# Weights split two blocks ahead instead of three, token copies in GpSimd's queue, and one softmax for four chunks

## The chip, the cores and the metric

The kernel runs on one core of a Trainium2 chip. The metric is the device time of one execution in microseconds (us). Five engines with a queue each work side by side: TensorE (PE; its weight loads are listed as PEld), VectorE (DVE), ScalarE (ACT), GpSimd (POOL) and SyncE (SP), which here only issues transfers. An engine takes its instructions in the order of its own queue, and a wait at the front of a queue holds back everything behind it.

## The reference

Two layers, each a mixer (a linear recurrence in layer 0, attention in layer 1) and a feed-forward part that picks experts, on 512 tokens of 1024 numbers. The change touches the feed-forward part, which is the same in both layers:

```python
def peer_ffn(h, q_w, subkey1, subkey2, expert_u, expert_v):     # for each chunk xc of 128 tokens
    q = (xc @ q_w).reshape(128, 8, 2, 128)
    s1, s2 = q[:, :, 0] . subkey1, q[:, :, 1] . subkey2          # 8 heads x 128 keys, twice
    v1, i1 = lax.top_k(s1, 16); v2, i2 = lax.top_k(s2, 16)
    cand = v1[..., :, None] + v2[..., None, :]                   # 256 sums for each head
    top_s, top_c = lax.top_k(cand, 16)
    expert = i1[top_c // 16] * 128 + i2[top_c % 16]              # one of 16384
    g = softmax(top_s)
    act = gelu(einsum('thkd,td->thk', expert_u[expert], xc))
    return einsum('thk,thkd->td', g * act, expert_v[expert])
```

## The kernel before

**Numbers in two parts.** Every product is made of three matmuls: a float32 operand is split into a rounded part (`hi`, ScalarE, line 189) and the rest (`lo`, VectorE, or GpSimd in one stage, line 191), and hi·hi, lo·hi and hi·lo are added in PSUM. Weights come in blocks of 128 x 1024 numbers. `Stream` loads two blocks with one transfer (SP), splits them one by one and hands them out with `take`. At a `take`, it first records the splits of all blocks up to `ahead` blocks beyond the one that is taken. The split parts (`whi`, `wlo`) live in a ring of four buffers, so the split of a block cannot start before TensorE is done with the block four places before it.

**The feed-forward part, `peer`.** Four chunks of 128 tokens. For chunks 0 to 2 all 16384 experts are computed (the dense way), with a gate that is zero for experts that weren't picked; the last 32 of these 384 tokens have their 128 products with `expert_u` looked up row by row instead (`looked_up`), so the dense products with `u` have 352 columns. Chunk 3 is looked up wholly (`gathered`). There are 128 expert blocks; for 34 of the 64 pairs of blocks the products with `u` are made early and stored in DRAM, for the other 30 within the last loop. The stages, one after the other:

1. Queries: scores, the 16 best of each side, the 16 best sums.
2. Routing: `route` finds for each chunk the expert numbers (`e1`, `e2`) and the softmax (`gt`) of the picked scores. For chunk 2 it also makes `ei`; then `looked_up` copies the indices of the 32 tokens to four groups of 32 partitions (`eix`, four small transfers), their rows of h to the same groups (`hn`, three transfers), fetches rows of `expert_u` by GpSimd (`rowx`, `two`), multiplies them on VectorE and copies the result back (`back`, four transfers).
3. Gates: `dense_gates` transposes `e1`, `e2` and `gt` on TensorE and builds the gate of every expert, beside the early products with `u`.
4. The expert sum: for each pair of blocks, VectorE multiplies the products by the gates (line 1332), ScalarE rounds them (`wh`, 1335), VectorE makes the rest (`wl`, 1340), and TensorE adds them times `v` (1347), 18 matmuls of 512 columns a block. If the pair six blocks on isn't stored, 24 matmuls of 352 columns for each of its blocks stand between (556 to 558). In the background VectorE works through chunk 3: 128 products with rows of `u` (`rows`, 1235), then 128 with rows of `v` (`accg`, 1249).

**What sets the order.** The program says what is to be done and what depends on what. A scheduler then orders the instructions of each engine by estimates of its own; only those marked `keep_in_program_order` keep their place among each other. `ahead` and the length of an instruction thus move others too.

## Time and profile before

| | |
|---|---|
| time, median of 3 runs | 3040.61 us (3040.06 to 3040.77) |
| profiled execution: time, span | 3042.44 us, 3040.4 us |
| PE busy | 2964.9 us (98%) |
| DVE busy | 2563.0 us (84%) |
| ACT busy | 1451.8 us (48%) |
| POOL busy | 1157.9 us (38%) |
| granted TensorE clock, mean | 0.992 |

In the profiled execution, layer 0's routing begins at about 438 us, its gates at 470, its expert sum at 720 (rows of `u` in the background until about 1120, then rows of `v`), and ends at 1464. Layer 1's come at 2000, 2030, 2280, 2680 and 3022.

A wait row reads: engine and line that waited, the instruction it waited for, us in total, how many times, the longest. A row of the windows reads: stretch, its length, the busy time of PE, PEld, DVE, ACT and POOL with counts, the granted TensorE clock (1.00 is full), the share of the DMA engines, GB/s. A timeline row: start, duration, engine, line, operation, tiles, and in brackets the idle time ahead of it and what ended it.

### The profile page before, as it was taken

What the parts mean: (1) busy time and instruction counts of PE and PEld (TensorE: products, weight loads), DVE (VectorE), ACT (ScalarE), POOL (GpSimd) and SP (SyncE); (2) the same over time, 40 slices, a digit from 0 to 9 for tenths busy, and PEclk for the clock granted to TensorE, in tenths of its full rate; (3) what the DMA queues carried; (4) which work ended last, traced back from release to release, by engine and by line L of the source; (5) the groups of instructions that cost most, each with busy time, mean ns of one, the idle gap of its engine ahead of it and who ended that gap; (6) DMA issues with size and microseconds to landing.
All of it is one profiled execution on the core that took longest, in us unless ns stands there. A gap on an engine that the chain in (4) does not pass through costs nothing.

```text
span 3040.4 us, 44431 instructions
## 1 busy us (share of the span) xinstructions
PE 2964.9 (98%) x16232; PEld 2605.4 (86%) x16232; DVE 2563.0 (84%) x4951; ACT 1451.8 (48%) x2300; POOL 1157.9 (38%) x906
## 2 busy tenths in 40 slices
PE   7999999999999999999999999999999999999998
PEld 5778899999888888888777778899998888888887
DVE  7876989995988888888779878899977898898887
ACT  6665564664333333333468843365663333333332
POOL 1002953201765645554011004631105565554551
PEclk9999999999999999999999999999999999999999
DMA  7455558998999999988332134377998999999995
GB/s 291 174 177 198 210 182 348 303 296 310 385 364 364 395 359 380 368 334 333 112 117 84 63 153 162 140 266 279 314 303 343 396 360 362 377 385 364 353 347 199
DMA packets 306843, 855.22 MB, mean 281 GB/s; under 512 B 26208, under 2 KB 161408, under 8 KB 267840
## 3 DMA queue, kind: packets, MB, share of 16 engines
q1 hardware_dynamic: 72464, 407.65, 35.2%
q0 software_dynamic: 93440, 336.11, 29.2%
q10 hardware_dynamic: 140720, 108.63, 10.8%
q8 instruction: 127, 2.08, 0.3%
q14 instruction: 92, 0.75, 0.1%
HBM read 767.93 MB, written 83.51 MB: 280 GB/s over the span
## 4 chain that ended last, share of the span: by engine, by line
PE 69%; DVE 16%; issue 8%; ACT 4%; DMA 2%; POOL 1%; DVEq 0%; ACTq 0%; SPq 0%; POOLq 0%
PE vacc L1347 27%; PE pacc L556 11%; PE pacc L557 10%; PE pacc L558 10%; DVE accg L1249 2%; PE gps L1179 2%; DVE wlo L191 2%; ACT whi L189 1%; DVE pg L1206 1%; DVE rows L1235 1%; DVE wl L1340 1%; PE oacc L600 1%; PE oacc L599 1%; PE oacc L601 1%; DMA wraw<-in_l_uT_dram 1%
## 5 line engine op out<-in xcount | busy, mean ns | idle before, releaser
L189 ACT ACTIVATE whi<-wraw 128x1024 fp32r<-128x1024 f32 (+1 forms) x646 | 669.0, 1039 | 893.8 <-PE vacc L1347 387.6
L191 DVE TENSOR_TENSOR wlo<-wraw,whi 128x1024 fp32r<-128x1024 f32 (+2 forms) x580 | 697.6, 1211 | 332.4 <-ACT whi L189 331.1
L556 PE MATMUL pacc<-hhi,whi 128*128 128x352 f32 (+1 forms) x2600 | 890.6, 343 | 0.6 <-issue 0.6
L558 PE MATMUL pacc<-hhi,wlo 128*128 128x352 f32 (+1 forms) x2600 | 883.1, 340 | 1.5 <-DVE wlo L191 1.5
L557 PE MATMUL pacc<-hlo,whi 128*128 128x352 f32 (+1 forms) x2600 | 882.8, 340 | 0.0
L1347 PE MATMUL vacc<-whi,wh 128*128 128x512 f32 x1536 | 601.0, 391 | 0.0
L1347 PE MATMUL vacc<-wlo,wh 128*128 128x512 f32 x1536 | 599.2, 390 | 0.0
L1347 PE MATMUL vacc<-whi,wl 128*128 128x512 f32 x1536 | 564.3, 399 | 22.0 <-DVE wl L1340 21.3
L557 PEld LDWEIGHTS pacc<-hlo,whi 128*128 128x128 f32 x2600 | 491.6, 189 | 26.6
L556 PEld LDWEIGHTS pacc<-hhi,whi 128*128 128x128 f32 x2600 | 490.3, 189 | 27.2 <-issue 0.9
L558 PEld LDWEIGHTS pacc<-hhi,wlo 128*128 128x128 f32 x2600 | 490.1, 188 | 26.3 <-DVE wlo L191 2.5
L1222 POOL DMA_INDIRECT rows<-in_l_v_dram,ei x256 | 369.6, 1444 | 348.0 <-DVE accg L1249 275.2
L1222 POOL DMA_INDIRECT rows<-in_l_u_dram,ei x256 | 409.3, 1599 | 242.7 <-DVE rows L1235 179.3
L1347 PEld LDWEIGHTS vacc<-whi,wl 128*128 128x128 f32 x1536 | 287.5, 190 | 100.3 <-DVE wl L1340 40.9
L1347 PEld LDWEIGHTS vacc<-whi,wh 128*128 128x128 f32 x1536 | 289.7, 189 | 57.5 <-ACT wh L1335 0.6
L1347 PEld LDWEIGHTS vacc<-wlo,wh 128*128 128x128 f32 x1536 | 290.0, 189 | 56.7
L1249 DVE SCALAR_TENSOR_TENSOR accg<-rows,act,accg 128x1024 f32<-128x1024 f32 x254 | 326.3, 1285 | 3.1
L1235 DVE SCALAR_TENSOR_TENSOR rows<-rows,hn 128x1024 f32<-128x1024 f32 x256 | 302.3, 1220 | 2.8 <-issue 2.8
L1335 ACT ACTIVATE wh<-at 128x768 fp32r<-128x768 f32 x128 | 108.2, 845 | 237.2 <-DVE at L1332 226.6
L191 POOL TENSOR_TENSOR wlo<-wraw,whi 128x1024 fp32r<-128x1024 f32 (+1 forms) x62 | 125.4, 2042 | 87.0 <-ACT whi L189 84.4
L1084 POOL DMA_INDIRECT rowx<-in_l_u_dram,eix x36 | 59.6, 1654 | 240.4 <-DVE rowx L1102 153.6
L1340 DVE TENSOR_TENSOR wl<-at,wh 128x768 fp32r<-128x768 f32 x128 | 121.8, 951 | 1.8 <-ACT wh L1335 1.8
(343 smaller groups left out, 3676.3 us busy)
## 6 DMA issues: line engine op xcount, KB each, us to landing
wraw<-in_l_uT_dram SPq DMA_DIRECT2D x128, 1024.0 KB
wraw<-in_l_vp_dram SPq DMA_DIRECT2D x128, 1024.0 KB
gscr<-st ACTq DMA_DIRECT2D x48, 1024.0 KB
gtile<-gscr SPq DMA_DIRECT2D x90, 512.0 KB
ascr<-at ACTq DMA_DIRECT2D x136, 176.0 KB
at<-ascr ACTq DMA_DIRECT2D x68, 352.0 KB
mw<-in_l_ffn_mw_dram POOLq DMA_DIRECT2D x32, 512.0 KB
wraw<-in_l_qw_dram SPq DMA_DIRECT2D x16, 1024.0 KB
```

The source lines that it names most:

```text
L189: self.pin(nc.scalar.activation(hi, raw, AF.Copy))
L191: self.pin((nc.gpsimd if self.on_pool else nc.vector).tensor_sub(lo, raw, hi))
L556: nc.tensor.matmul(ps, whi[:, k, :], hhi[:, k, :n], start=(k == 0), stop=False))
L557: nc.tensor.matmul(ps, whi[:, k, :], hlo[:, k, :n], start=False, stop=False)
L558: nc.tensor.matmul(ps, wlo[:, k, :], hhi[:, k, :n], start=False, stop=(k == KD - 1))
L1179: m = T.matmul(gps[:, r, :], p2[:, tk_, :, :].rearrange("p a b -> p (a b)"), pg[:, i].rearrange("p a (t b) -> p a t b", b=8)[:, :, tk_, :] ...
L1222: i = nc.gpsimd.indirect_dma_start(out=rows, out_offset=None, in_=src, in_offset=bass.IndirectOffsetOnAxis(ap=ei[:, j:j + 1], axis=0))
L1235: V.scalar_tensor_tensor(r, r, 1.0, hn, op0=OP.mult, op1=OP.mult, accum_out=act[:, j:j + 1]))
L1249: i = V.scalar_tensor_tensor(acc, r, w, acc, op0=OP.mult, op1=OP.add)
L1335: (pin if c < 2 else lambda x: x)(A.activation(wh, at, AF.Copy))
L1340: return lambda: pin(V.tensor_sub(wl, at, wh))
L1347: T.matmul(acc[t][d], x[:, ts], y[:, d, :], start=(i == 0 and x is wh and y is vh), stop=(i == PK - 1 and x is wl))
```

## The change

Three edits, in both layers:

- `ahead` stays at two for the expert sum's loop and goes back to three only behind it. (The gate stage had two before.)
- The copies of `eix`, `hn` and `back` are issued in GpSimd's queue, not in ScalarE's: eleven transfers in each layer.
- The softmax is made once for all four chunks, when the first chunk has been routed: one subtraction, one exponential, one sum and one reciprocal of four times the length; the last multiplication stays with each chunk.

```diff
+        def weights():
+
+            ex = env["exp"] = rs.tile([128, TC, PH, TOPK], F32, name="exps")
+            V.tensor_tensor(ex, top, top[:, :, :, 0:1].to_broadcast([128, TC, PH, TOPK]), op=OP.subtract)
+            A.activation(ex, ex, AF.Exp)
+            gs = env["sum"] = rs.tile([128, TC, PH], F32, name="sums")
+            V.tensor_reduce(gs, ex, axis=AX.X, op=OP.add)
+            V.reciprocal(gs, gs)
+
         def route(t):
...
             e = routes[t]
+            if t == nd - 1:
+                weights()
             gt = (rt if t < nd else pk).tile([128, PH, TOPK], F32, name="gt", tag="gt_", bufs=3 if t < nd else 1)
-            V.tensor_tensor(gt, top[:, t], top[:, t, :, 0:1].to_broadcast([128, PH, TOPK]), op=OP.subtract)
-            A.activation(gt, gt, AF.Exp)
-            gs = rt.tile([128, PH], F32, name="gs", tag="gs")
-            V.tensor_reduce(gs, gt, axis=AX.X, op=OP.add)
-            V.reciprocal(gs, gs)
-            V.tensor_tensor(gt, gt, gs.unsqueeze(2).to_broadcast([128, PH, TOPK]), op=OP.mult)
+            V.tensor_tensor(gt, env["exp"][:, t], env["sum"][:, t].unsqueeze(2).to_broadcast([128, PH, TOPK]), op=OP.mult)
...
             def groups(to, of):
                 for s in range(SG):
-                    nc.scalar.dma_start(to[s * XT:(s + 1) * XT], of[own, s * XT:(s + 1) * XT])
+                    nc.gpsimd.dma_start(to[s * XT:(s + 1) * XT], of[own, s * XT:(s + 1) * XT])
...
             for s in range(SG - 1):
-                nc.scalar.dma_start(hn[s * XT:(s + 1) * XT], hn[own])
+                nc.gpsimd.dma_start(hn[s * XT:(s + 1) * XT], hn[own])
...
             for s in range(SG):
-                nc.scalar.dma_start(back[own, s * XT:(s + 1) * XT], act[s * XT:(s + 1) * XT])
+                nc.gpsimd.dma_start(back[own, s * XT:(s + 1) * XT], act[s * XT:(s + 1) * XT])
...
                     bg.pump(GP)
                 bg.finish()
-                g.stream.ahead = 3
...
             bg.finish()
+            g.stream.ahead = 3
             gguard.__exit__(None, None, None)
```

**The order at the expert sum.** VectorE's queue in layer 0, in the part with rows of `v`, ahead of one `wl`. A block's two parts are `whi_N` and the `wlo` numbered one higher; numbers grow in the order of the program and differ between the two builds. Before, where `wl_12416` belongs to the pair that begins with block 12383:

```order
L1249 SCALAR_TENSOR_TENSOR accg_8337<-rows_12417,act_8336,accg_8337 128x1024
L191 TENSOR_TENSOR wlo_12421<-wraw_12381,whi_12420 128x1024
L191 TENSOR_TENSOR wlo_12427<-wraw_12424,whi_12426 128x1024
L1249 SCALAR_TENSOR_TENSOR accg_8337<-rows_12451,act_8336,accg_8337 128x1024
L1249 SCALAR_TENSOR_TENSOR accg_8337<-rows_12454,act_8336,accg_8337 128x1024
L1249 SCALAR_TENSOR_TENSOR accg_8337<-rows_12457,act_8336,accg_8337 128x1024
L191 TENSOR_TENSOR wlo_12496<-wraw_12424,whi_12495 128x1024
L1249 SCALAR_TENSOR_TENSOR accg_8337<-rows_12460,act_8336,accg_8337 128x1024
L1340 TENSOR_TENSOR wl_12416<-at2_12250,wh_12414 128x768
```

The same place in the changed kernel, where `wl_12396` belongs to the pair that begins with block 12402:

```order
L1255 SCALAR_TENSOR_TENSOR accg_8319<-rows_12397,act_8318,accg_8319 128x1024
L191 TENSOR_TENSOR wlo_12403<-wraw_12400,whi_12402 128x1024
L191 TENSOR_TENSOR wlo_12407<-wraw_12400,whi_12406 128x1024
L1255 SCALAR_TENSOR_TENSOR accg_8319<-rows_12431,act_8318,accg_8319 128x1024
L1255 SCALAR_TENSOR_TENSOR accg_8319<-rows_12434,act_8318,accg_8319 128x1024
L1255 SCALAR_TENSOR_TENSOR accg_8319<-rows_12437,act_8318,accg_8319 128x1024
L191 TENSOR_TENSOR wlo_12478<-wraw_12475,whi_12477 128x1024
L1255 SCALAR_TENSOR_TENSOR accg_8319<-rows_12440,act_8318,accg_8319 128x1024
L1345 TENSOR_TENSOR wl_12396<-at2_12230,wh_12394 128x768
```

The kinds of instructions are the same; each split is now that of the block one place earlier (before, those of blocks one, two and three behind 12383; now those of 12402 itself and the next two).

TensorE's queue at the block that first needs this `wl`, before:

```order
L1347 MATMUL vacc20_8067<-whi_12383,wh_12414 128x512
L1347 MATMUL vacc20_8067<-wlo_12384,wh_12414 128x512
L1347 MATMUL vacc21_8068<-whi_12383,wh_12414 128x512
L1347 MATMUL vacc21_8068<-wlo_12384,wh_12414 128x512
L1347 MATMUL vacc00_8063<-whi_12383,wl_12416 128x512
L1347 MATMUL vacc01_8064<-whi_12383,wl_12416 128x512
```

and now:

```order
L1352 MATMUL vacc00_8049<-whi_12402,wh_12394 128x512
L1352 MATMUL vacc00_8049<-wlo_12403,wh_12394 128x512
L1352 MATMUL vacc01_8050<-whi_12402,wh_12394 128x512
L1352 MATMUL vacc01_8050<-wlo_12403,wh_12394 128x512
L1352 MATMUL vacc10_8051<-whi_12402,wh_12394 128x512
L1352 MATMUL vacc00_8049<-whi_12402,wl_12396 128x512
```

Before, all twelve matmuls of the block that don't need `wl` stood ahead of the first that does; now five do. There are 64 `wl` in each layer; the rows `wlo`, three times `accg`, `wlo`, `accg`, `wl` stand ahead of one seven times in each layer, before and now.

**The order at routing.** ScalarE's queue in layer 0, before:

```order
L876 ACTIVATE at<-pacc 128x352
L1003 ACTIVATE tab_4802<-d_4798 128x1024
L877 DMA ascr<-at 128x352
L1065 DMA eix<-ei 32x32 x4
L299 ACTIVATE hn<-nat 128x512 x2
L876 ACTIVATE at<-pacc 128x352
L1092 DMA hn<-hn 32x1024 x3
L877 DMA ascr<-at 128x352
L189 ACTIVATE whi<-wraw 128x1024
```

and now:

```order
L189 ACTIVATE whi<-wraw 128x1024
L876 ACTIVATE at<-pacc 128x352
L1003 ACTIVATE tab_4805<-idxs_2606 128x1024
L877 DMA ascr<-at 128x352
L299 ACTIVATE hn<-nat 128x512 x2
L1003 ACTIVATE tab_4803<-d_4799 128x1024
L189 ACTIVATE whi<-wraw 128x1024
```

The seven transfers are gone from between `hn` and the next weight split, `whi`; in GpSimd's queue they now stand ahead of and among the first `rowx`. TensorE's queue at the first transposes of the gate stage, before:

```order
L556 MATMUL pacc_5028<-hhi_2330,whi_4941 128x352
L557 MATMUL pacc_5028<-hlo_2331,whi_4941 128x352
L1158 MATMUL tp_5796<-ident_86,e0_4795 128x128
L1158 MATMUL tp_5796<-ident_86,e1_4796 128x128
L558 MATMUL pacc_5028<-hhi_2330,wlo_4942 128x352
```

and now:

```order
L558 MATMUL pacc_5742<-hhi_2330,wlo_5659 128x352
L1164 MATMUL tp_5782<-ident_86,e0_4796 128x128
L1164 MATMUL tp_5782<-ident_86,e1_4797 128x128
L1164 MATMUL tp_5782<-ident_86,gt_5096 128x128
L556 MATMUL pacc_5801<-hhi_2330,whi_5702 128x352
```

The transposes of `e1` and `e2` of chunk 0 stand 430 rows later now, beside that of its `gt`, which kept its place.

## The prediction

> **What bounds the kernel now.** I began with the page's busy rows and groups, then took the waits of TensorE stage by stage, the timeline of one place at which it waits, and the windows behind such places.

> ```profile
> PE 2964.9 (98%) x16232; PEld 2605.4 (86%) x16232; DVE 2563.0 (84%) x4951; ACT 1451.8 (48%) x2300; POOL 1157.9 (38%) x906
> L1347 PE MATMUL vacc<-whi,wl 128*128 128x512 f32 x1536 | 564.3, 399 | 22.0 <-DVE wl L1340 21.3
> ```

> TensorE is busy for 98% of the span of 3040.4 us, and none of the edits removes a matmul. So the change can only be worth what TensorE loses in the stages that it touches. The second row names the largest such loss: 21.3 us of waiting for `wl`. The waits of TensorE in the two expert sums (720 to 1464 and 2280 to 3022) place it:

> ```profile
> PE vacc L1347 <- DVE wl L1340: 10.4, 6, 3.0
> PE vacc L1347 <- DVE wl L1340: 10.9, 7, 2.7
> ```

> What makes `wl` late is seen in the timeline of the place whose order is shown above, with the rows of PE, ACT and DVE:

> ```profile
> 1237.64 0.39 PE L1347 MATMUL vacc<-whi,wh 128*128 128x512 f32 x1
> 1244.21 0.39 PE L1347 MATMUL vacc<-wlo,wh 128*128 128x512 f32 x1
> 1247.62 0.50 PE L1347 MATMUL vacc<-whi,wl 128*128 128x512 f32 x1 [3.02 <-DVE wl L1340]
> 1238.17 1.06 ACT L189 ACTIVATE whi<-wraw 128x1024 fp32r<-128x1024 f32 x1 [2.43 <-issue]
> 1239.27 1.22 DVE L191 TENSOR_TENSOR wlo<-wraw,whi 128x1024 fp32r<-128x1024 f32 x1 [3.08 <-ACT whi L189]
> 1240.41 3.92 DVE L1249 SCALAR_TENSOR_TENSOR accg<-rows,act,accg 128x1024 f32<-128x1024 f32 x3
> 1244.24 1.22 DVE L191 TENSOR_TENSOR wlo<-wraw,whi 128x1024 fp32r<-128x1024 f32 x1
> 1245.38 1.32 DVE L1249 SCALAR_TENSOR_TENSOR accg<-rows,act,accg 128x1024 f32<-128x1024 f32 x1
> 1246.62 0.94 DVE L1340 TENSOR_TENSOR wl<-at,wh 128x768 fp32r<-128x768 f32 x1
> ```

> At 1237.64 TensorE begins a block, and so frees the buffer of the block before. ACT can then split into it (1238.17), DVE idles 3.08 us for that, makes `wlo` (1239.27), four `accg`, another `wlo`, and only then `wl` (1246.62). TensorE goes on at 1247.62, 9.98 us after it freed the buffer. It wanted to at 1244.21 + .23 = 1244.44, since matmuls of 512 columns start .2267 us apart in these rows. So DVE wasn't short of time before this; a split that could not start sooner stood ahead of `wl`.

> The windows tell what follows a wait: stretch, length, then PE, PEld, DVE, ACT, POOL and the granted clock.

> ```profile
> 1244.40:1247.70 3.30, 0.28 (x2) 0.08 (x1) 3.30 (x4) 0.04 (x1) 2.41 (x3) 1.00 1.01 412
> 1248.90:1252.40 3.50, 3.50 (x10) 2.72 (x9) 3.46 (x4) 1.47 (x2) 2.19 (x2) 0.51 1.02 426
> 1358.10:1361.60 3.50, 3.50 (x10) 2.73 (x9) 3.08 (x4) 1.90 (x2) 1.98 (x2) 0.51 0.90 345
> 1443.40:1446.90 3.50, 3.49 (x8) 2.75 (x9) 3.30 (x3) 1.43 (x2) 0.00 (x0) 0.51 0.55 234
> 2808.80:2812.30 3.50, 3.50 (x10) 2.74 (x9) 3.25 (x4) 1.90 (x2) 1.98 (x2) 0.51 1.02 425
> 2918.00:2921.50 3.50, 3.23 (x8) 2.58 (x9) 3.46 (x4) 1.37 (x3) 1.98 (x2) 0.51 0.89 324
> 3003.40:3006.90 3.50, 3.08 (x8) 2.47 (x8) 3.46 (x4) 0.96 (x2) 0.00 (x0) 0.51 0.64 260
> ```

> Behind each of the three longest waits of each layer the granted clock is .51 for 3.50 us, while TensorE is busy. That costs 3.50 x .49 = 1.71 us each, 6 x 1.71 = 10.3 us in all, which the waits don't count. [...]

> **The change: splits two blocks ahead.** The same row of instructions stands on DVE ahead of `wl`, seven times in each layer, so from the release of the buffer to TensorE's start I keep 9.98 us. The split that begins it is now that of one block nearer, whose buffer comes free one block sooner as seen from the block that is running. Before, TensorE had from the release one block of 18 matmuls and 12 of the next until it wanted `wl`: 18 x .2267 + 12 x .2267 = 6.80 us. Now it has two blocks and five matmuls, as the second pair of order rows shows: 36 x .2267 + 5 x .2267 = 9.29 us. The wait at such a place falls from 3.18 to 9.98 − 9.29 = .69 us. I take it for all 14 places: 14 x .69 = 9.7 us remain, and 21.3 − 9.7 = 11.6 us go. The ends are 0 left (21.3 saved) and, if the four places in each layer that hardly wait now keep to that, and the scheduler's other changes undo half of it, some 6 us saved. A wait of .7 us is far below the 2.5 us or so behind which dips stand, so the six dips go: **10.3 us**. For that the window at the other end is evidence: the 1.6 us wait at 2624.5 leaves the clock at 1.00.

> ```profile
> 2624.50:2628.00 3.50, 3.46 (x16) 2.92 (x17) 3.13 (x4) 1.36 (x3) 2.03 (x2) 1.00 0.96 363
> ```

> The other face of this edit is that splits have one block less of lead. The nearest rows are a pair of splits and the block that needs it:

> ```profile
> 824.85 2.35 DVE L191 TENSOR_TENSOR wlo<-wraw,whi 128x1024 fp32r<-128x1024 f32 x2
> 827.65 0.32 PE L556 MATMUL pacc<-hhi,whi 128*128 128x352 f32 x1
> ```

> The pair ends .45 us before TensorE needs it. I take 0 for its loss, since such splits wait for the release of their buffer and not for their place in the program; the other end is one `wlo` late at each of the 60 pairs that aren't stored, and is a rival below.

> **Routing.** The waits of TensorE at 438 to 470 (three rows) and at 2000 to 2030 (two), and what ACT does ahead of the first:

> ```profile
> PE tp L1158 <- DVE e L989: 1.6, 1, 1.6
> PE pacc L558 <- DVE wlo L191: 0.8, 1, 0.8
> PE pacc L556 <- issue: 0.6, 1, 0.6
> PE tp L1158 <- DVE ge L986: 2.5, 1, 2.5
> PE pacc L558 <- DVE wlo L191: 0.7, 1, 0.7
> 450.88 2.56 ACTq L1065 DMA_DIRECT2D eix<-ei  x4
> 454.60 3.12 ACTq L1092 DMA_DIRECT2D hn<-hn  x3
> 458.41 1.06 ACT L189 ACTIVATE whi<-wraw 128x1024 fp32r<-128x1024 f32 x1 [3.48 <-issue]
> 463.80:467.30 3.50, 3.50 (x15) 3.50 (x14) 3.50 (x6) 0.15 (x1) 3.03 (x2) 0.51 1.04 410
> 2020.30:2027.20 6.90, 6.12 (x20) 5.83 (x21) 6.62 (x10) 0.88 (x1) 5.68 (x5) 0.51 1.01 393
> ```

> The seven issues hold ACT for 2.56 + 3.12 = 5.68 us, and the next weight split starts behind them after 3.48 us without work; TensorE waits .6 for it. Then the transposes of the experts' numbers stand ahead of the products and wait 1.6 and 2.5 us for VectorE, which also puts `wlo` behind. Now the issues have left ACT, and the transposes stand 430 rows later, where their `gt` had kept the gates anyway. I take all five waits, 1.6 + .8 + .6 + 2.5 + .7 = 6.2 us, and the two dips: 3.50 x .49 = 1.7 and 6.90 x .49 = 3.4. The dips are 5.1 us; together **11.3 us**. The low end is 0, if DVE's work reaches TensorE late by another way.

> **The copies in GpSimd's queue.** No such small copy is issued by POOL before. The nearest rows are its issues of other plain transfers, and its indirect fetches, with min, median and max in ns:

> ```profile
> L217 POOL DMA_DIRECT2D mw<-in_l_ffn_mw_dram x32 | 17.2, 538 | 197.7 <-DVE mw L224 131.8 <-DVE col_l_ffn L231 28.3 <-DVE ptl L304 22.8
> L1084 POOL DMA_INDIRECT rowx<-in_l_u_dram,eix x36: 936/1331/2752, 455.5 to 2160.8; - x36
> 455.54 1.15 POOL L1084 DMA_INDIRECT rowx<-in_l_u_dram,eix  x1 [32.24 <-DMA eix<-ei]
> 462.76 1.22 DVE L1102 SCALAR_TENSOR_TENSOR rowx<-rowx,hn 128x1024 f32<-128x1024 f32 x1
> ```

> Eleven issues at .54 us are 6 us a layer, in a queue that stood idle 32.24 us ahead of the first `rowx`. Behind the `hn` copies stand the fetches, and behind the fetches only the products `rowx` on DVE. Three `hn` copies among three fetches, at .54 and 1.33 us, take 5.6 us from 455.5 on: they are out at about 461, and DVE came to its first `rowx` at 462.76. So I take 0. At 2.75 us, the longest of these rows, the six would end at 472; DVE would stand some 9 us at `rowx` with splits queued behind, and the 11.3 us of routing would go back. [...]

> **One softmax.** It saves three of four rounds in each layer:

> ```profile
> L1044 ACT ACT_TABLE_LOAD x8 | 10.3, 1283 | 0.1
> ```

> Six table loads of 1.28 us go from ACT, which is busy 48%, and some short operations from DVE. No wait of TensorE above names either; 0, and with the ACT cover gone at most 6 x 1.28 = 7.7 us of gain.

> **Sum.** 11.6 + 10.3 + 11.3 = 33.2 us. The profiled execution took 3042.44 us, 1.83 above the median of 3040.61 (2.0 around its span). 3042.4 − 33.2 = 3009.2; against the median, 3040.6 − 33.2 = **3007 us**. If all that is listed went, 21.3 + 10.3 + 11.3 = 42.9, it would be 2998.

> **Rivals.**

> *VectorE is the bound at these places.* While TensorE waits, DVE is busy for 3.30 of 3.30 us (first window). Were its work simply too much there, a sooner release would only move the wait, dips included, and routing alone would gain: 3040.6 − 11.3 = 3029. For it speaks the row of the rows-of-`v` stretch:

> ```profile
> 1120.00:1464.00 344.00, 335.03 (x1601) 287.87 (x1600) 293.17 (x261) 122.17 (x164) 163.05 (x116) 0.99 0.89 342
> ```

> Against it: 293 of 344 us is 85%, and the idle 3.08 us stands directly ahead of the long run.

> *Nothing comes of it.* As before, and the copies by POOL take 2.75 us, so that routing gives back its gain as well; that is about 3040, at most a few us below.

> *Slower: splits come late.* With one block less of lead each pair that isn't stored finds its second `wlo` behind one more DVE instruction, 1.22 us, of which the .45 us of margin covers a part: .77 us at 60 pairs is 46 us, minus the 33 gained: 3053. It decides from a mean lateness of 33.2 / 60 = .55 us. For it speaks the thin margin; against it, that TensorE shows no wait for `wlo` in either expert sum, and that DVE idles for `whi`, which comes by release.

> *All of it goes:* 2998, if the four other places in each layer catch up and the .69 us is covered.

> **How the numbers follow.** Chances: the forecast .62, DVE as the bound .15, nothing .08, slower .10, all of it .05. Within 0.2%, 6.1 us, a measurement of this kernel can hardly be told from no change. Faster by more come the forecast, DVE as the bound and all of it: .82; the same .08; slower .10. The range goes from 2997, all of it, to 3031, which takes in DVE as the bound: .62 + .15 + .05 = .82. The forecast's own range is 3000 to 3018.

> **What would show it.** Right: the waits for `wl` sum to some 10 us, none over 1 us; no window of clock .51 in either expert sum; no wait at the transposes; the first `rowx` on DVE near 463. Wrong: waits of 2.5 us and dips at the same count (DVE the bound); new waits of `pacc` for `wlo` in the expert sums (slower); DVE idle at `rowx` for a DMA (the copies). What I couldn't price from any row is how else the scheduler moves instructions once lengths change.

## The result, and the profile after

The changed kernel takes 2996.53 us (median of 4 runs, 2995.56 to 3000.91), where the kernel before took 3040.61. The ratio is 0.9858, with a 95% interval of 0.9841 to 0.9875: 38 to 48 us less. The forecast was 3007 us with a range down to 2997; the time lies half a microsecond below that end, and next to the rival "all of it goes" (2998), though not by that rival's way, as is shown below.

The page's busy rows of the changed kernel, and its row for the products that waited for `wl`:

```profile
PE 2943.4 (98%) x16232; PEld 2597.3 (87%) x16232; DVE 2560.1 (86%) x4933; ACT 1436.0 (48%) x2282; POOL 1196.9 (40%) x928
L1352 PE MATMUL vacc<-whi,wl 128*128 128x512 f32 x1536 | 594.7, 391 | 0.9
```

TensorE does the same 16232 matmuls, and the 21.3 us of waiting for `wl` are no longer there. The span is 46.6 us shorter (3040.4 to 2993.8). Where from is seen if both traces are cut at the same instructions: the first score product of the queries, the first product with `v`, and the last.

| us | before | after |
|---|---|---|
| layer 0: queries, routing, gates | 429.1 | 427.4 |
| layer 0: expert sum | 753.3 | 733.7 |
| layer 1: queries, routing, gates | 430.8 | 427.6 |
| layer 1: expert sum | 753.4 | 733.6 |

The expert sums gave 19.6 + 19.8 = 39.4 us, routing and gates 1.7 + 3.2 = 4.9. The rest, some 2 us, lies at the start and in the mixers, which the change doesn't touch; 1.7 of it is a dip of the clock at 1822 that is gone (last section). The expert sums end at 1475 and 3035 before, 11 and 13 us later than the stage times given ahead. Their windows, before:

```profile
721.00:1475.00 754.00, 743.28 (x3592) 641.16 (x3591) 635.36 (x712) 274.53 (x371) 395.76 (x268) 0.99 0.91 352
2281.00:3035.00 754.00, 742.72 (x3592) 641.05 (x3591) 633.07 (x704) 269.46 (x358) 391.85 (x265) 0.99 0.91 351
```

and after:

```profile
718.00:1452.00 734.00, 733.51 (x3590) 638.00 (x3590) 634.61 (x712) 273.65 (x370) 406.05 (x268) 1.00 0.93 360
2254.00:2988.00 734.00, 733.54 (x3590) 637.96 (x3589) 631.73 (x704) 268.69 (x358) 404.57 (x265) 1.00 0.93 360
```

VectorE does the same work (635.36 and 634.61 us) in 20 us less, and TensorE is busy throughout, at the full clock. So VectorE's load was not the bound.

The place whose order stands in the chapter on the change, in the timeline of the changed kernel, rows of PE, ACT and DVE:

```profile
1224.51 0.39 PE L1352 MATMUL vacc<-whi,wh 128*128 128x512 f32 x1
1233.59 0.39 PE L1352 MATMUL vacc<-whi,wh 128*128 128x512 f32 x1
1234.01 0.50 PE L1352 MATMUL vacc<-whi,wl 128*128 128x512 f32 x1
1224.55 1.06 ACT L189 ACTIVATE whi<-wraw 128x1024 fp32r<-128x1024 f32 x1 [2.11 <-PE pacc L557]
1225.64 1.23 DVE L191 TENSOR_TENSOR wlo<-wraw,whi 128x1024 fp32r<-128x1024 f32 x1 [1.95 <-ACT whi L189]
1226.79 3.92 DVE L1255 SCALAR_TENSOR_TENSOR accg<-rows,act,accg 128x1024 f32<-128x1024 f32 x3
1230.63 1.22 DVE L191 TENSOR_TENSOR wlo<-wraw,whi 128x1024 fp32r<-128x1024 f32 x1
1231.76 1.32 DVE L1255 SCALAR_TENSOR_TENSOR accg<-rows,act,accg 128x1024 f32<-128x1024 f32 x1
1233.01 0.95 DVE L1345 TENSOR_TENSOR wl<-at,wh 128x768 fp32r<-128x768 f32 x1
```

From `whi` to TensorE's first matmul with `wl` it still takes 9.46 us (before 9.45). What changed is that this chain begins when two blocks and five matmuls lie ahead of that matmul. It is .2 us late here (1234.01, where 1233.59 + .23 = 1233.82 would be prompt), not 3.18.

Routing and the gates are where less came than forecast. The waits of TensorE there, two in each layer, and the windows behind the second of each:

```profile
PE gps L1185 <- DVE pg L1212: 2.1, 1, 2.1
PE pacc L558 <- DVE wlo L191: 0.7, 1, 0.7
PE gps L1185 <- DVE pg L1212: 1.9, 1, 1.9
PE pacc L558 <- DVE wlo L191: 1.2, 1, 1.2
538.20:541.60 3.40, 3.40 (x28) 3.40 (x26) 3.40 (x5) 2.53 (x5) 0.47 (x1) 0.54 0.55 169
2074.20:2077.60 3.40, 3.30 (x33) 3.30 (x32) 3.40 (x6) 1.79 (x3) 0.00 (x0) 0.54 0.49 131
```

The waits at the transposes are gone, but two others are not. The first gate product now waits 2.1 and 1.9 us (1.1 before in both layers), and the clock halves behind it in both layers. And a split is still late, by .7 and 1.2 us (.8 and .7 before), in layer 0 by this chain of rows of POOL, DVE and PE:

```profile
458.80 0.57 POOL L1098 DMA_DIRECT2D hn<-hn  x1
465.00 1.23 DVE L1108 SCALAR_TENSOR_TENSOR rowx<-rowx,hn 128x1024 f32<-128x1024 f32 x1 [1.23 <-DMA hn<-hn]
471.95 1.22 DVE L191 TENSOR_TENSOR wlo<-wraw,whi 128x1024 fp32r<-128x1024 f32 x1
473.23 0.43 PE L558 MATMUL pacc<-hhi,wlo 128*128 128x352 f32 x1 [0.65 <-DVE wlo L191]
```

GpSimd issued the last copy of `hn` in .57 us and was done at 459.4 (the prediction had 461), but VectorE could start on it only at 465.0, some 5.6 us after the issue ended. VectorE stood 1.23 us for it (1.88 in layer 1), then another .41 and .47 us for rows fetched for `two`, and the `wlo` that TensorE waits for stands behind these.

### The profile page after: what moved, and what is told of

The parts are those of the page before. It is cut to its first block, busy times and chain, and to the rows that moved or that the text cites. A ratio compares the mean times of both kernels' runs of the same rounds, so it can differ in the third digit from the quotient of the medians.

```text
span 2993.8 us, 44407 instructions
## 1 busy us (share of the span) xinstructions
PE 2943.4 (98%) x16232; PEld 2597.3 (87%) x16232; DVE 2560.1 (86%) x4933; ACT 1436.0 (48%) x2282; POOL 1196.9 (40%) x928
## 3 DMA queue, kind: packets, MB, share of 16 engines
q10 hardware_dynamic: 139664, 107.77, 11.3%
## 4 chain that ended last, share of the span: by engine, by line
PE 74%; DVE 13%; issue 6%; ACT 3%; DMA 2%; POOL 1%; DVEq 0%; SPq 0%; ACTq 0%; POOLq 0%
PE vacc L1352 32%; PE pacc L556 10%; PE pacc L557 10%; PE pacc L558 10%; PE gps L1185 2%; DVE wlo L191 2%; DVE pg L1212 1%; DVE accg L1255 1%; ACT whi L189 1%; DMA mw<-in_l_mix_mw_dram 1%; PE oacc L601 1%; PE oacc L600 1%; PE oacc L599 1%; DMA two<-in_l_u_dram,eix 1%; DVE rowx L1108 1%
## 5 line engine op out<-in xcount | busy, mean ns | idle before, releaser
L189 ACT ACTIVATE whi<-wraw 128x1024 fp32r<-128x1024 f32 (+1 forms) x646 | 668.7, 1038 | 906.5 <-PE pacc L557 423.5
L191 DVE TENSOR_TENSOR wlo<-wraw,whi 128x1024 fp32r<-128x1024 f32 (+2 forms) x580 | 697.2, 1211 | 287.7 <-ACT whi L189 283.3
L556 PE MATMUL pacc<-hhi,whi 128*128 128x352 f32 (+1 forms) x2600 | 889.4, 342 | 0.0
L558 PE MATMUL pacc<-hhi,wlo 128*128 128x352 f32 (+1 forms) x2600 | 882.4, 340 | 2.0 <-DVE wlo L191 1.9
L1352 PE MATMUL vacc<-whi,wl 128*128 128x512 f32 x1536 | 594.7, 391 | 0.9
L558 PEld LDWEIGHTS pacc<-hhi,wlo 128*128 128x128 f32 x2600 | 489.0, 188 | 29.0 <-DVE wlo L191 6.6
L1228 POOL DMA_INDIRECT rows<-in_l_u_dram,ei x256 | 419.9, 1640 | 230.0 <-DVE rows L1241 165.6
L556 PEld LDWEIGHTS pacc<-hhi,whi 128*128 128x128 f32 x2600 | 489.5, 188 | 25.6 <-ACT at L876 0.2
L1228 POOL DMA_INDIRECT rows<-in_l_v_dram,ei x256 | 382.0, 1492 | 317.9 <-DVE accg L1255 249.2
L1255 DVE SCALAR_TENSOR_TENSOR accg<-rows,act,accg 128x1024 f32<-128x1024 f32 x254 | 325.9, 1283 | 2.9
L1340 ACT ACTIVATE wh<-at 128x768 fp32r<-128x768 f32 x128 | 108.4, 846 | 196.4 <-DVE at L1337 186.5
L191 POOL TENSOR_TENSOR wlo<-wraw,whi 128x1024 fp32r<-128x1024 f32 (+1 forms) x62 | 124.8, 2026 | 85.4 <-ACT whi L189 82.7
```

The source lines that it names most:

```text
L189: self.pin(nc.scalar.activation(hi, raw, AF.Copy))
L191: self.pin((nc.gpsimd if self.on_pool else nc.vector).tensor_sub(lo, raw, hi))
L556: nc.tensor.matmul(ps, whi[:, k, :], hhi[:, k, :n], start=(k == 0), stop=False))
L558: nc.tensor.matmul(ps, wlo[:, k, :], hhi[:, k, :n], start=False, stop=(k == KD - 1))
L1228: i = nc.gpsimd.indirect_dma_start(out=rows, out_offset=None, in_=src, in_offset=bass.IndirectOffsetOnAxis(ap=ei[:, j:j + 1], axis=0))
L1255: i = V.scalar_tensor_tensor(acc, r, w, acc, op0=OP.mult, op1=OP.add)
```

## Experiments: which edit does it

**The first edit alone.**

```diff
 (kernel before)
                 bg.finish()
-                g.stream.ahead = 3
 ...
             bg.finish()
+            g.stream.ahead = 3
             gguard.__exit__(None, None, None)
```

> Only the first edit. Theory A (the late release of the split's buffer is what made wl late): the two expert sums lose what they lost in the changed kernel, 753.3 to some 734 us each, so 2 x 19.6 = 39 us: 3001 us, no wait for wl over 0.5 us, no window of clock 0.51 in either expert sum; routing as before, with its five waits and its dips. Rival B (the other two edits, by moving instructions, made room on VectorE): the waits for wl stay near 21 us and the time is over 3025 us.

Measured: 3002.45 us, ratio 0.9879 (0.9863 to 0.9896), 32 to 42 us gained. The expert sums took 733.6 and 733.5 us; their windows:

```profile
724.00:1458.00 734.00, 733.57 (x3597) 638.21 (x3596) 634.90 (x713) 273.52 (x370) 395.85 (x268) 1.00 0.94 360
2262.00:2995.00 733.00, 732.58 (x3586) 637.30 (x3587) 631.27 (x703) 268.21 (x357) 398.65 (x265) 1.00 0.93 360
```

Theory A holds: this edit by itself takes the waits for `wl` and the dips out. Routing and gates stay at 429.7 and 430.6.

**The change without the first edit**, three blocks ahead again, the other two edits kept.

> The changed kernel with three blocks ahead in the expert sum again. Theory A: 39 us come back, 3036 us, with some 13 waits for wl (21 us) and six dips of the clock. Rival B: under 3012 us, waits for wl mostly gone.

Measured: 3031.32 us, ratio 0.9972 (0.996 to 0.9983). The waits for `wl` in the two expert sums are back, and five dips with them (a sixth wait had none):

```profile
PE vacc L1353 <- DVE wl L1346: 8.7, 5, 2.7
PE vacc L1353 <- DVE wl L1346: 10.9, 9, 2.7
```

It came out some 5 us below the expectation. The expert sum of layer 0 took 749.8 us, not 753.3, and that of layer 1 753.5; so the other edits moved something in layer 0 too, a little.

**The second edit alone**: `nc.gpsimd.dma_start` for `nc.scalar.dma_start` at the eleven copies, nothing else.

> Only the second edit; the first transposes of the gate stage move back by 430 rows with it, as in the change. Theory A: what the two layers gained from the start of the queries to the end of the gates, some 5 us, and nothing else: 3035 us; VectorE waits about 1.2 us for the copy of hn, the waits at the transposes are gone, a wait of some 2 us at the first gate product takes their place. Rival (the copies by GpSimd cost more than ACT's issues did): 3041 us or more.

Measured: 3033.47 us, ratio 0.9981 (0.9972 to 0.9991): 3 to 9 us gained. Queries to gates took 427.5 and 428.2 us, as in the changed kernel, the expert sums 752.1 and 751.9. The expected wait at the first gate product did not come; the waits of `pacc` for `wlo` in routing came to 4.9 us instead.

**The change with the copies back in ScalarE's queue**, so the first and the third edit.

> The changed kernel with the eleven copies in ScalarE's queue again; the transposes stay where the change has them. Theory C (the queue edit gains nothing by itself, the move of the transposes gained): 2994 to 2998 us, no wait of VectorE for hn. Rival D (the seven issues on ACT hold back whi and TensorE): TensorE waits 0.5 us or more for a split in each layer, and dips follow: 2999 to 3003 us.

Measured: 3008.11 us, ratio 0.9903 (0.9887 to 0.992), above both expectations; the profiled span was 3002.3, 8.5 us over the changed kernel's. Queries to gates took 430.7 and 432.9 us (427.4 and 427.6), the expert sums 733.4 and 733.6. So rival D holds: the queue edit does gain. In the timeline of layer 0, rows of ACT, DVE and PE:

```profile
453.55 3.10 ACTq L1098 DMA_DIRECT2D hn<-hn  x3
458.34 2.01 ACT L189 ACTIVATE whi<-wraw 128x1024 fp32r<-128x1024 f32 x2 [0.54 <-ACT at L876]
463.49 1.22 DVE L1108 SCALAR_TENSOR_TENSOR rowx<-rowx,hn 128x1024 f32<-128x1024 f32 x1 [0.87 <-DMA rowx<-in_l_u_dram,eix]
464.64 1.22 DVE L191 TENSOR_TENSOR wlo<-wraw,whi 128x1024 fp32r<-128x1024 f32 x1
465.91 0.43 PE L558 MATMUL pacc<-hhi,wlo 128*128 128x352 f32 x1 [3.95 <-DVE wlo L191]
```

The issues hold `whi` back to 458.34; the `wlo` of a later block then falls behind a `rowx` on VectorE that waits for its own rows. With the transposes out of the way TensorE runs into this wait of 3.95 us (3.98 in layer 1) instead of theirs. How much of it is the late `whi` and how much the place of the `wlo` behind `rowx`, these rows don't tell.

**The third edit alone**: one softmax for four chunks.

> Only the third edit. The transposes of the gate stage move back with it too. Theory C (its own cost or gain is only in that move; with ACT's seven issues still there TensorE waits for splits in place of the transposes, as in the run with the copies back in ScalarE's queue): from the start of the queries to the end of the gates 430.7 and 432.9 us as there, 3.6 more than before, expert sums as before at 753: 3044 us, a ratio of 1.001. Rival (one softmax frees VectorE and ScalarE for the routing): below 3035 us, a ratio under 0.998.

Measured: 3042.28 us, ratio 1.0009 (0.9999 to 1.0018): no gain. Queries to gates took 430.3 and 431.8 us, with `pacc` waits for `wlo` of 8.0 us, the longest 4.4: theory C holds there. The expert sums took 751.8 and 748.5 us, the second 4.9 less than before, with two of its three dips gone (2806.9 and 2915.4 have the wait and no dip); theory C had not said so.

**The change without the third edit**, so the first two.

> The changed kernel with a softmax for each chunk, so the first two edits. Theory C: the same as the changed kernel within 2 us (expert sums 734 us, queries to gates as with the queue edit alone, 427.5 and 428.2): ratio 0.985 to 0.987. Rival (the softmax carries part of the gain): over 0.988.

Measured: 2997.64 us, ratio 0.9861 (0.9845 to 0.9877), the same as the changed kernel within the noise: no gain of the softmax can be seen. The expert sums took 733.9 and 733.8 us. Queries to gates took 424.1 and 429.4 us, not the 427.5 and 428.2 expected: without the third edit layer 0 was faster than in the changed kernel and layer 1 slower.

## Experiments: the release of the buffer

The first two runs show that `ahead` does it, not why. The theory says that the split's buffer came free too late; the rival, that the split stood too early in VectorE's queue. A fifth buffer frees it sooner at the same `ahead`.

**Five split buffers, paid for with row buffers (inconclusive).** In the kernel before, every fifth block of the expert sum is split into a buffer of its own, and eight buffers for looked-up rows become six. Its control has the six row buffers alone.

> The kernel before, three blocks ahead, but a ring of five buffers for the split parts in the expert sum (every fifth block in a buffer of its own), paid for by six row buffers for the looked-up rows in place of eight. Theory A (the release of the buffer is what is late): a split three ahead now waits for the block five places before it, which is released one block sooner, as with two ahead and four buffers: the waits for wl fall below 5 us, no dips in the expert sums, some 39 us gained beside its control: ratio about 0.988. Rival E (what counts is where the split stands in VectorE's queue, not when its buffer is free): waits for wl near 20 us, ratio over 0.995.

> Control of the run with five buffers: the kernel before with six row buffers in place of eight and four split buffers. Theory A: the waits for wl stay near 20 us; between 3038 and 3046 us (fewer rows in flight gain nothing), ratio 0.999 to 1.002. Rival: if fewer row buffers alone move the waits for wl below 10 us, the run with five buffers shows nothing.

Measured: 3036.47 us with five split buffers (ratio 0.9988, 0.9976 to 1.0) and 3058.94 for the control (1.0062, 1.0046 to 1.0079). The pair shows nothing on the question. With six row buffers alone the waits for `wl` in the part with rows of `v` fell to 2.6 and 2.3 us, as the rival of the control had it, but those in the part with rows of `u` rose to 15.3 and 16.7, which neither it nor the expectation had. Besides, VectorE waited 9.1 and 7.7 us for a transfer of the gate stage (`gscr`) ahead of a split, once in each layer; that the added buffer took over memory which this transfer still read is my reading.

**Five split buffers, paid for with a raw weight buffer.** All row buffers stay, and the fifth buffer is used from the fifth pair until 16 blocks before the end:

```diff
 (kernel before)
-            sp = self.spare or g.wsp
+            sp = self.spare or (self.fifth if len(self.parts) % 5 == 4 else None) or g.wsp
 ...
-            g.stream.third = (pk, vw)
+            g.stream.third = (pk,)
 ...
+                if i == 8:
+                    g.stream.fifth = fifth
                 if i == PK - 16:
                     g.stream.third = None
+                    g.stream.fifth = None
```

> The kernel before, three blocks ahead, with a fifth buffer for the split parts from the fifth pair of the expert sum on; all eight row buffers stay, and it is paid for by the raw weight buffer that the last stage had in addition (three in place of four). Theory A (the buffer's late release is the cause): in the part with rows of v (1120 to 1464, 2680 to 3022) the waits for wl fall from 8.7 and 8.4 us to under 2, without dips; expert sums some 15 us shorter each than in its control; ratio about 0.989. Rival E (the place of the split in VectorE's queue): waits there of 7 us or more, as before, ratio over 0.996.

The control has three raw buffers and four split buffers:

> Control of the run with five split buffers: the kernel before with three raw weight buffers in the expert sum in place of four. Theory A: waits for wl in the parts with rows of v stay at 8 us, with dips; 3038 to 3045 us. Rival: waits for a weight load appear (over 5 us), or the waits for wl there move below 4 us by themselves; then the pair shows nothing.

Measured: 3021.68 us with the fifth buffer (ratio 0.995, 0.9934 to 0.9967), 3040.14 for the control (1.001, 0.9999 to 1.0021). The expert sums took 742.1 and 742.4 us against 751.2 and 753.2. The waits of TensorE in the parts with rows of `v` (1110 to 1460, 2660 to 3010), control first, then with five buffers:

```profile
PE vacc L1347 <- DVE wl L1340: 8.4, 4, 2.7
PE vacc L1347 <- DVE wl L1340: 8.9, 5, 2.7
```

```profile
PE vacc L1349 <- DVE wl L1342: 2.7, 1, 2.7
PE vacc L1349 <- DVE wl L1342: 2.7, 1, 2.7
```

Two of the three long waits of each layer are gone, and the one that remains, in layer 0 at 1428 to 1431, lies where the ring is back to four. A window around the second place, control first, then with five buffers, and behind it the window with the wait that remains:

```profile
1345.00:1360.00 15.00, 12.26 (x55) 9.82 (x54) 12.32 (x11) 4.29 (x5) 7.62 (x6) 1.00 0.87 316
```

```profile
1345.00:1360.00 15.00, 14.96 (x70) 12.21 (x69) 14.91 (x14) 6.17 (x8) 10.32 (x7) 1.00 0.97 354
1420.00:1440.00 20.00, 17.30 (x70) 13.79 (x69) 14.96 (x15) 5.22 (x6) 1.71 (x4) 0.91 0.64 246
```

VectorE's queue did not change at three of these four places: at both in layer 0, and at the first in layer 1, the same row stands ahead of `wl` (`wlo`, three `accg`, `wlo`, `accg`), as in the control. What changed is how long its first split waits, here at the second place, control first, then with five buffers:

```profile
1347.57 1.23 DVE L191 TENSOR_TENSOR wlo<-wraw,whi 128x1024 fp32r<-128x1024 f32 x1 [2.79 <-ACT whi L189]
```

```profile
1337.54 1.23 DVE L191 TENSOR_TENSOR wlo<-wraw,whi 128x1024 fp32r<-128x1024 f32 x1 [1.95 <-ACT whi L189]
```

So at the same `ahead` and the same order a buffer that is free sooner removes the wait: theory A, by its mechanism, and not rival E. The gain, some 10 us a layer, is less than the 15 expected, since one place of three kept its wait and waits of up to 2.5 us came up in the part with rows of `u`, one with a dip behind it (2326.6). The ratio fell between the two theories' numbers.

**One block ahead.** The changed kernel with `g.stream.ahead = 1` set behind the gate stage.

> The changed kernel with splits only one block ahead in the expert sum. Theory A and F (splits wait for release and VectorE's turn, and there is margin left at two): expert sums within 2 us of 734, about 2997 us. Rival of the prediction (splits come late with less lead, 0.77 us at each of the 60 pairs that aren't stored): 46 us slower than the changed kernel, some 3040 us, with waits of TensorE for wlo in the expert sums.

Measured: 2987.83 us, ratio 0.984 (0.9824 to 0.9856). The rival of the prediction, late splits, falls: no wait for `wlo` or `wl` is left in either expert sum, and they are another 4.6 us shorter each (729.0), more than my expectation had. The window of layer 0's:

```profile
717.70:1448.00 730.30, 730.30 (x3599) 640.27 (x3600) 634.80 (x715) 274.33 (x370) 412.64 (x268) 1.00 0.93 362
```

TensorE doesn't pause once. This is the fastest version measured, though its interval and the changed kernel's overlap.

**The copies of `hn` in SyncE's queue**, in the changed kernel.

> The changed kernel with the three copies of hn in SyncE's queue, eix and back in GpSimd's. If VectorE's 1.2 us at the first rowx come from GpSimd's slow copy: VectorE's wait there goes, TensorE's waits for wlo of 0.9 and 1.4 us in routing go with it, and the time is 2 to 4 us below the changed kernel: 2993 us, ratio 0.984 to 0.985. If SyncE's loads hold the copies back: VectorE waits over 2 us at the first rowx, 2997 us or more.

Measured: 3004.95 us, ratio 0.9899 (0.9883 to 0.9916), span 2998.9; a miss. Queries to gates took 429.8 and 429.6 us. VectorE no longer waits for `hn`, but for the rows that are multiplied with it:

```profile
457.83 1.20 POOL L1090 DMA_INDIRECT rowx<-in_l_u_dram,eix  x1 [5.39 <-DMA eix<-ei]
462.57 1.22 DVE L1108 SCALAR_TENSOR_TENSOR rowx<-rowx,hn 128x1024 f32<-128x1024 f32 x1 [3.58 <-DMA rowx<-in_l_u_dram,eix]
468.31 1.22 DVE L191 TENSOR_TENSOR wlo<-wraw,whi 128x1024 fp32r<-128x1024 f32 x1
PE pacc L558 <- DVE wlo L191: 3.9, 1, 3.9
```

The first fetch starts at 457.83, 3.5 us later than in the changed kernel, after GpSimd waited for the indices. Why these landed later I haven't settled. VectorE reaches its first `rowx` ahead of the data and stands 3.58 us there and 1.41 at the second; the `wlo` that TensorE needs stands behind them (468.31), and TensorE waits 3.9 us.

## Why the prediction was right, and where it was off

- **What bounds it.** Right: TensorE's waits behind a late split, not VectorE's load. One edit alone and the fifth buffer show it.
- **Term 1, the waits for `wl`, 11.6 us.** Mis-sized: all 21.3 us went. The step that failed is ".69 us at all 14 places". Before, only six of them were late, by 2.9 to 3.2 us (16.6 us of the 21.3 in wait rows; 4.7 stood elsewhere), and the other eight by .16; after, all 14 are late by .20 to .26. At the place shown, the chain of 9.46 us stood, but it began earlier: `whi` started .04 us after TensorE began the next block (1224.51, 1224.55), where it took .53 before (1237.64, 1238.17). The block that frees the buffer is now one with products with `u`, and `whi` is released by a matmul (557) that isn't its last. So .2 us were left, which no wait row lists.
- **Term 2, the dips, 10.3 us.** Right: no window of .51 is left in either expert sum.
- **Not in the sum.** The expert sums gave 39.4 us, and the two terms in full are 21.3 + 10.3 = 31.6. The other 7.8 us were in no row that I had read; those were wait rows of TensorE's matmuls alone. Its weight loads have wait rows too, before and after:

```profile
PEld vacc L1347 <- DVE wl L1340: 40.9, 55, 3.4
```

```profile
PEld vacc L1352 <- DVE wl L1345: 9.5, 22, 0.5
```

  A load that comes late by a little delayed its matmul without a wait row of the matmul's own: in the changed kernel 22 loads wait for `wl`, none over .53 us, while no matmul in the expert sums has a wait row; at the place shown the load waited .46 us, and its matmul started .20 late. Measured by the starts of the matmuls against their steady distance, the time lost in the two expert sums fell from 50.3 us to 10.9: delays over .3 us from 24.5 to none (the waits' rows hold 21.3 of them), smaller ones, dips included, from 25.8 to 10.9. So the 7.8 us are 3.2 of long delays beyond their rows (a row begins where the matmul before is taken to end: 3.02 us in the row, 3.18 by the starts) and 4.6 of small ones. With one block ahead no weight load waits for `wl` in the expert sums, and by the same measure 1.6 us are lost.
- **Term 3, routing, 11.3 us.** Too large: 4.9 us came. Two steps failed. "The transposes stand 430 rows later, where their `gt` had kept the gates anyway" left the first gate product out; it waits 1.0 and .8 us longer, and a dip followed each time, which costs 3.40 x .46 = 1.6 us. And "so I take 0" for the copies: they were issued in time, but the issue isn't the landing. With that, waits for `wlo` of .7 and 1.2 us stayed, where the term had all of them gone. Together 1.8 + 3.2 + 1.9 = 6.9 us, about the 6.4 that are missing.

  Each of the second and third edits alone moves the transposes back by the same 430 rows; the first alone doesn't. But the move doesn't lengthen the wait at the gate product by itself. In the eight kernels that have it, that wait goes with what TensorE lost in routing before: it is .9 to 1.0 us in the nine layers where TensorE had waited 1.9 us or more for a split, and 1.4 to 2.1 in the seven where it had waited 1.3 or less. Both stand in one kernel, the change without the third edit: .4 us and then 1.4 in layer 0, 4.2 and then .9 in layer 1. So about a microsecond of what TensorE wins in routing is given back at the gate product, which waits for VectorE's `pg`. This is read from the traces; no run moved `pg` alone.
- **The softmax, 0.** Right within the noise, by both runs.
- **The rivals.** VectorE as the bound: refuted. Late splits: refuted, as even one block ahead is enough. The slow copies: the 9 us at `rowx` were 1.23 and 1.88. The issue of the last copy took .57 us, and VectorE could start some 5.6 us after its end; no run shows what these 5.6 us consist of. All of it goes: the number is close, the way is not. Of the 42.9 us listed there routing kept 6.4, and the 7.8 and 2.3 us that came in addition were not listed; 42.9 − 6.4 + 7.8 + 2.3 = 46.6 us of span.

So the expert sums gave some 17 us more than forecast and routing 6 less, which left the forecast 10 us high. That the errors have opposite signs, and that the time came so near the end of the range, is luck; the mechanism of the first edit is not.

## What to carry to other kernels

How far ahead a split is queued and how many buffers it has belong together: an instruction that waits for a buffer holds up what stands behind it on its engine, so queueing it earlier than the buffer can be free makes other work late (here VectorE's 3.08 us at a split, and 3.02 us of TensorE's at the `wl` behind it). Look at the weight loads' wait rows beside the matmuls', and at the starts of matmuls, since small delays add up to as much as a term of the sum (25.8 us before, 10.9 after). Price a moved transfer by when its data lands, not by its issue (here .57 us for the issue, some 5.6 us more until VectorE could start). And when a wait goes, look at the next place where the engine meets another engine: part of the gain can be lost there.

## What the runs showed of the hardware

```profile
1821.76 0.59 PE L542 MATMUL pacc<-hhi,whi 128*128 128x352 f32 x2 [2.49 <-DVE hhi L489]
1818.96:1822.38 3.42, 0.93 (x6) 0.40 (x4) 3.28 (x9) 1.72 (x4) 0.00 (x0) 1.00 0.72 287
1822.30:1825.70 3.40, 3.40 (x12) 3.35 (x12) 2.51 (x6) 3.34 (x7) 0.57 (x1) 0.51 0.00 0
```

and after:

```profile
1799.00 0.59 PE L542 MATMUL pacc<-hhi,whi 128*128 128x352 f32 x2 [2.49 <-DVE hhi L489]
1794.55:1797.96 3.41, 1.92 (x16) 1.44 (x14) 3.38 (x6) 2.42 (x5) 0.00 (x0) 1.00 0.51 168
1797.96:1801.38 3.42, 2.38 (x13) 2.09 (x14) 2.86 (x9) 1.78 (x4) 0.00 (x0) 1.00 0.33 139
1799.50:1805.00 5.50, 5.50 (x34) 5.27 (x34) 4.43 (x12) 5.28 (x11) 0.59 (x1) 1.00 0.00 0
```

Before, the whole wait lies in one window, in which TensorE is busy for .93 of 3.42 us. After, it lies across the border of two, with 1.92 and 2.38 us. In the control with three raw buffers one of the six long waits for `wl`, 2.74 us, passed without a dip in the same way, across a border:

```profile
1355.93 0.50 PE L1347 MATMUL vacc<-whi,wl 128*128 128x512 f32 x1 [2.74 <-DVE wl L1340]
1351.46:1354.87 3.41, 1.73 (x8) 1.11 (x6) 3.41 (x3) 0.17 (x1) 2.62 (x3) 1.00 0.56 172
1355.70:1362.70 7.00, 6.77 (x30) 5.61 (x31) 6.93 (x7) 3.15 (x4) 4.59 (x4) 1.00 0.97 355
```

Summed from the matmul rows of all fourteen traces, window by window of the grid from 60 us on, TensorE's busy time went with the dips almost without fail. After a window at the full clock with TensorE busy for less than 44% of it, the clock was halved in the next one 72 times of 72; after one of more than 57%, never in 11922; between the two, 13 times of 36. In the traces of before and after alone these are 11 of 11, none of 1702 and none of 4. A dip ended after a window that was over 85% busy (85 of 85) and went on for another after one under 83% (14 of 14); before, the one that went on has TensorE busy for 2.68 of 3.41 us in its first window (2020.35 to 2023.76). So the dips lasted 3.41 us or a multiple of it: from 60 us on eight of 3.41 and one of 6.83 before, two of 3.41 after, beside the one that each trace ends in. Busy time is modelled here, which may be why the border isn't sharp, and no run moved a wait against the windows on purpose: this is read from the traces, not tested.

Ahead of these eleven dips TensorE waited 1.9 to 3.0 us, once in two waits of 1.55 and .81 us (at 461.76 and 462.90 before), and was busy for .67 to 1.49 us of the window that ended where the dip began. So less was enough than the 2.5 us or so of the prediction. For a sum it means that a dip, about 1.7 us (3.41 x .5), depends on where the wait falls, as at line 542, and may come or stay away with a shift of the program.
